# Narrow products as column tiles of the array: HGRN2's levels within 32 tokens and Mamba-2's chunk products

## The chip, the core and the metric

The kernel runs on one core of one Trainium2 chip. TensorE (PE) multiplies and writes to PSUM, VectorE (DVE) and ScalarE (ACT) do elementwise work, GpSimd (POOL) a few small operations, and SyncE (SP) issues nearly all transfers. The metric is the device time of one execution in microseconds, as the median of several runs.

## What is computed

The reference is an encoder trunk of two layers on 512 tokens of 1024 features. Layer 0 mixes tokens with HGRN2, layer 1 with Mamba-2, both in both directions, and each is followed by a gated channel mixer (ConvGLU). What the change touches are the products within a block of tokens:

```python
# HGRN2, one direction, per chunk (b = cumulated log of the forget gate)
rel = jnp.where(lower, b[t] - b[s], -inf)
att = jnp.einsum('bhtsk,bhsk->bhts', qc * jnp.exp(rel), kc)
o = o_inter + jnp.einsum('bhts,bhsv->bhtv', att, vc)
# Mamba-2, one direction, per chunk of 128
cb = jnp.einsum('bclgn,bcsgn->bgcls', cc, bc)
y_diag = jnp.einsum('bgjcls,bcsgjp->bclgjp', cb[:, :, None] * lmat, xd)
```

Everything is float32; HGRN2 has 8 heads of 128 channels, Mamba-2 32 heads of 64 channels in 8 groups.

## The kernel before

**Projections.** All large products take both operands split into two float32r parts and sum three products (`mm3`, lines 160 to 162), mostly 128 x 128 x 512. The weights come in pieces through `load`; ACT copies the high part (L134) and DVE subtracts the low part (L135).

**The order on TensorE** in the two mixers is written out by hand. A generator of projection work (`fill`) yields its cost, and `weave` inserts the steps of each head or group among it at given times (`HEADS` and `HSTEPS` for HGRN2, `MAMBA` and `STEPS` for Mamba-2). The orders on the other engines come from the framework's scheduler.

**HGRN2, a head (`mix(hd)`).** The tile `kq` holds four arrays of 128 channels x 512 tokens: the keys and queries of both directions. The attention within a block of 128 tokens is built by halving. The diagonal (`p0`, L537) and then levels m = 1, 2, 4, 8, 16, 32, 64 each take one step. At level m, ACT gathers into `km` the forward keys of each block's first half and the backward keys of the second (L545), TensorE multiplies it with the gathered queries over whole blocks of 128 x 128, four of them in one PSUM bank `pl` (L551), and of these DVE keeps with a masked copy those pairs that part at this level (L554 for the diagonal, L556), in the tile `at0` of 128 x 512. At m = 64 there is no mask: two products of 64 x 64 for each block go to the two halves of the partitions (L560, L562), and ACT copies them (L564, L565). After each level DVE multiplies the level's decays into `kq` in place (L574, L575), which the next level's gather and products wait for, and forms the decays of the doubled blocks (`tot`, L577). At the end `at0` is the left operand of the head's output (L612).

**Mamba-2, a group (`mix(g)`).** For each of four heads, `weights(j)` makes C B^T with decays and step sizes (ACT L879, DVE L881 and L883) as a tile E of 128 x 512, and L933 multiplies each block of 128 x 128 with the head's 64 channels of `x_t`, into 64 columns of `py`. L939 follows, the product with the states.

**Norms.** `stats` sums the squares over the channels with products against one column of ones (L225), after each mixer and channel mixer and in the last output.

Of the kernel before, what the change touches and what calls it, by code (L numbers as in the profile page):

```python
# [9 lines left out]
F32 = mybir.dt.float32  # L10
# [8 lines left out]
P = 128  # L19
T = 512  # L20
NB = T // P
# [10 lines left out]
# when HGRN2's heads are worked on among its projections, and the steps of a head, of 13 in all  # L32
HEADS = ((66, 136), (90, 170), (133, 209), (169, 250), (213, 292), (248, 315), (293, 353), (314, 368))
HSTEPS = (1, 1, 2, 3, 4, 5, 6, 7, 8.3, 9.5, 10, 11, 12)
# Mamba-2's work for TensorE, in order: a group's projections of B, C and x, its z, and parts of the output
MAMBA = [(c[0], int(c[1:])) for c in "p0 z0 p1 z1 p2 z2 o1 p3 o1 z3 o2 p4 z4 o2 p5 z5 o2 p6 z6 p7 z7 o8".split()]
# when the steps of a group's scan are issued among it, from the start of its projections
# [4 lines left out]
# artanh(s) = s (1 + z p(z)), z = s^2, to 4e-10 of it on |s| <= 1/3  # L42
# [3 lines left out]
def fl(t):  # L46
    """A tile [P, a, b] as [P, a*b]."""
    return t.rearrange("p a b -> p (a b)")


def view(ap, offset, dims):
    """The elements of ap's partitions at `offset` from its first, by [stride, size] pairs."""
    return bass.AP(tensor=ap.tensor, offset=ap.offset + offset, ap=[ap.ap[0], *dims])
# [3 lines left out]
def tile_trunk(ctx: ExitStack, tc: tile.TileContext, x, norm1_w, norm2_w, a_w_in, a_lb_logits, a_norm_w, a_w_out,  # L57
# [24 lines left out]
    # residual stream, channel-major, and the operand of the next projection split in two  # L82
# [22 lines left out]
    def bmask(m):  # L105
        return m.unsqueeze(1).to_broadcast([P, NB, P])

# [1 line left out]
    plan, ready = deque(), deque()  # L109

    def want(key, parts, nk):
        """Queues the columns of `parts` (APs of nk * 128 rows), side by side."""
        for k0 in range(0, nk, 4):
            plan.append((key, [x[k0 * P:min(nk, k0 + 4) * P] for x in parts]))
# [28 lines left out]
    def take(key, ahead=2):  # L143
        """The next weights in the plan, and those after them on their way."""
        got = []
        while (ready or plan) and (ready[0][0] if ready else plan[0][0]) == key:
            if not ready:
                k, parts = plan.popleft()
                ready.append((k, halves(*load(parts))))
            got.append(ready.popleft()[1])  # L150
        assert got, key
        fetch(ahead)

        def part(i, k, c0, n=P):
            return got[k // 4][i][:, k % 4, c0:c0 + n]

        return part
# [6 lines left out]
    # Streams of work for TensorE are generators that yield the time (in products of 128 x 128 x 512) of each piece.  # L164
    def proj_ch(p, w, c0):
        """Channel-major projection of the normalized stream (before its row scale): [128 features, T]."""
        yield from proj_chs([(p, w, c0)])

    def proj_chs(ps):
        """Several of them side by side, while the stream's tiles come in."""  # L170
        for k in range(ND):
            for p, w, c0 in ps:
                mm3(p, w(0, k, c0), w(1, k, c0), uhi[k], ulo[k], k == 0, k == ND - 1)
            if k % 2:
                yield 2 * len(ps)

    def proj_tok(p, w, blks):
        """Token-major projection of two blocks of tokens: [128 tokens, 2, 256 features]."""
        for i, b in enumerate(blks):
            bs = slice(b * P, b * P + P)  # L180
            for k in range(ND):
                mm3(p[:, i * 256:(i + 1) * 256], uhi[k][:, bs], ulo[k][:, bs], w(0, k, 0, 256), w(1, k, 0, 256),
                    k == 0, k == ND - 1)
                if k % 4 == 3:
                    yield 2

    def weave(fill, jobs, t=0):
        """Runs `fill`, and among it the steps of each job (steps, times), each at its time."""
        todo = sorted(((t, i) for i, (_, times) in enumerate(jobs) for t in times), reverse=True)
        for c in fill:  # L190
            t += c
            while todo and todo[-1][0] <= t:
                next(jobs[todo.pop()[1]][0], None)
        while todo:
            next(jobs[todo.pop()[1]][0], None)
# [24 lines left out]
    def stats(tmp, blocks=range(NB), more=()):  # L220
        """The tokens' scales, from the squares' sums and tiles of more squares."""
        pst = misc_ps()
        for b in blocks:
            for n, s in enumerate((ssum, *more)):
                PE.matmul(pst[:, b:b + 1], s[:, b * P:(b + 1) * P], ones[:, 0:1], start=n == 0, stop=n == len(more))  # L225
# [5 lines left out]
    def spread(tmp):  # L231
        """The tokens' scales along the free axis."""
# [7 lines left out]
    def out_proj(key, yhi, ylo, after):  # L240
        """h += w^T y, and `after` for each finished tile."""
# [98 lines left out]
    def first_masks():  # L340
        """Masks on [s, t] of a 128-block: the pairs that part at a level of halving."""
# [4 lines left out]
        xf = ip.tile([P, P], F32, name="xf")  # L346
        ge = ip.tile([P, P], F32, name="ge")
        V.tensor_tensor(mU, si, ti, ALU.is_le)
        V.tensor_tensor(si, si, ti, ALU.bitwise_xor)
        V.tensor_copy(xf, si)  # L350
        masks[0] = cst.tile([P, P], U8, name="m0")
        V.tensor_scalar(masks[0], xf, 0.0, None, ALU.is_equal)
        for m in (2, 4, 8, 16, 32):
            masks[m] = cst.tile([P, P], U8, name=f"m{m}")
# [3 lines left out]
    def params():  # L358
# [4 lines left out]
        # lower bounds of the forget gate: softmax over the layers' logits, first row  # L363
# [20 lines left out]
    def come(*ds):  # L384
        """Tiles of x, channel-major in PSUM."""
# [66 lines left out]
    def hgrn2():  # L452
# [66 lines left out]
        def mix(hd):  # L519
# [8 lines left out]
            # attention within blocks of 128, [s, t]; between them, states [k channel, v channel]  # L528
            at0 = t2k("at0", 2)
            diag = pv(at0)  # L530
# [4 lines left out]
            for b in range(NB):  # L535
                bs = slice(b * P, b * P + P)
                PE.matmul(p0[:, bs], ks[:, bs], q[:, bs], start=True, stop=True)  # L537
# [3 lines left out]
            while m < P:  # L541
                n2 = T // (2 * m)
                if m < 64:
# [3 lines left out]
                    pl = misc_ps()  # L547
                    for b in range(NB):
                        bs = slice(b * P, b * P + P)
                        qm = view(kq, T + b * P, [[2 * m, P // (2 * m)], [T + m, 2], [1, m]])  # L550
                        PE.matmul(pl[:, bs], km[:, bs], qm, start=True, stop=True)  # L551
                    if m == 1:
                        A.copy(diag, pv(pl))
                        V.copy_predicated(diag, bmask(masks[0]), pv(p0))  # L554
                    else:
                        V.copy_predicated(diag, bmask(masks[m]), pv(pl))  # L556
                else:
                    pl = misc_ps()
# [7 lines left out]
                # from blocks of m to blocks of 2m  # L566
# [14 lines left out]
            # tot: [P, 2, NB], products over blocks of 128; the blocks whose states the next ones (before, backward) take  # L581
# [23 lines left out]
            # output of the head, its norm and gate  # L605
# [26 lines left out]
        # a pair's projections take 80 units, the first six heads' output 48  # L632
# [71 lines left out]
    def mamba():  # L704
# [35 lines left out]
        def steps(x1):  # L740
            """Step sizes and cumulated decays: rows (half of the tokens, direction, head)."""
# [3 lines left out]
            # softplus: max(x, 0) + log1p(e), e = exp(-|x|); log1p(e) = 2 artanh(e / (2 + e)), at most 2 artanh(1/3)  # L745
# [88 lines left out]
        def h4(ap):  # L834
            """[P, n, 4 heads x 64] with the heads apart."""
            return ap.rearrange("p n (h e) -> p n h e", e=64)

        def mix(g):
            sb, sc, sx0, sx1, z = groups[g]
            hs = 4 * g  # L840
            # token-major x and B, and C B^T within the chunks as [s, l]
# [23 lines left out]
            def hv(t, c0, n, dr):  # L865
                """Per token and head, spread over a head's channels: [P, n, 4, 64]."""
                return t[:, c0:c0 + n, dr * NH + hs:dr * NH + hs + 4].unsqueeze(3).to_broadcast([P, n, 4, 64])

            def weights(j):
                """C B^T with the decays and step sizes of a head, as [s, l]."""  # L870
# [16 lines left out]
            # states at the chunks' borders  # L887
# [27 lines left out]
            # diagonal of the backward direction and the skip: one factor per token and head  # L915
# [10 lines left out]
            # within the chunks, a head at a time, and among them what the states give  # L926
            py = [misc_ps(), misc_ps()]
            for j in range(4):
                yield
                w = ws[j]  # L930
                for b in range(NB):
                    o = (b % 2) * 256 + j * 64
                    PE.matmul(py[b // 2][:, o:o + 64], w[:, b * P:(b + 1) * P], x_t[:, b, j * 64:(j + 1) * 64],  # L933
                              start=True, stop=True)
# [14 lines left out]
            # gate and group norm  # L949
# [68 lines left out]
        # a group's step begins with its projections of B, C and x (32 units, 8 more for the first group's dt)  # L1018
# [20 lines left out]
    def last_out(key, yhi, ylo, pool):  # L1039
        """The last products, the norm, and the output; the last tiles by halves of the tokens."""  # L1040
# [3 lines left out]
        def finish(d, p, ts, blocks):  # L1044
            """The tile's last steps; those of TensorE are left for later."""
# [79 lines left out]
```

## Time and profile before

| | |
|---|---|
| median of 3 runs | 1607.37 us (1607.34 to 1609.07) |
| profiled execution, span from first to last instruction | 1605.7 us |
| TensorE matmul busy / weight loads busy | 1589.4 / 1339.1 us |
| VectorE / ScalarE / GpSimd busy | 1060.1 / 773.5 / 27.4 us |
| matmuls | 8239 |
| HBM read / written | 147.70 / 2.23 MB |

The profile is of one execution, and its times are from its first instruction to its last; the median of the runs is 1.7 us above its span. Matmuls overlap in the array, so that their durations add up to more than the time they take: a matmul's price is the distance from its start to the next one's. A line such as L160 is that of the helper `mm3`, for all projections. The tensors' names in the rows are the program's: `pp` and `pm` are PSUM tiles of projections and of the rest.

### The profile page before, as it was taken

The page shows a single profiled execution, that of the slowest core. Times are in us where ns is not written, and L with a number is a line of the kernel's source. Part 1 is how long each engine was busy: PE and PEld are TensorE (multiplying, and loading weights), DVE is VectorE, ACT ScalarE, POOL GpSimd, SP SyncE. Part 2 cuts the span into 40 slices and gives each one's busy share as a digit, 9 for nine tenths or more (in the row PEclk, how much of TensorE's full clock was granted, in tenths as well). Part 3 has the DMA queues.
Part 4 walks back from the last instruction along what each step waited for, and adds up shares of the span by engine and source line. Part 5 has one row for each costly group of instructions (what it writes and reads, how often), then busy time and mean ns, then how long its engine had stood idle before and what let it go on. Part 6 is the DMA issues. An engine that isn't in the chain of part 4 may idle for free.

```text
span 1605.7 us, 21165 instructions
## 1 busy us (share of the span) xinstructions
PE 1589.4 (99%) x8239; PEld 1339.1 (83%) x8239; DVE 1060.1 (66%) x1652; ACT 773.5 (48%) x1356; POOL 27.4 (2%) x31
## 2 busy tenths in 40 slices
PE   8999999999999999999999999999999999999998
PEld 6889898987888888887888888888887888888887
DVE  6687677777655345545898888787878655246543
ACT  5445444535433123333589876667755333123333
POOL 0000000000000000000000000000000000000000
PEclk9999999999999999999999999999999999999999
DMA  5312222113232333323254334334313323233221
GB/s 180 101 53 67 66 66 66 47 44 113 87 101 83 105 92 92 99 79 99 77 172 135 116 109 119 120 93 117 101 47 118 96 89 105 79 105 95 82 81 71
DMA packets 153579, 151.31 MB, mean 94 GB/s; under 512 B 8374, under 2 KB 144263, under 8 KB 153479
## 3 DMA queue, kind: packets, MB, share of 16 engines
q1 hardware_dynamic: 153415, 149.93, 30.5%
q8 instruction: 65, 1.06, 0.3%
q14 instruction: 35, 0.29, 0.1%
q0 software_dynamic: 32, 0.02, 0.0%
q10 hardware_dynamic: 32, 0.01, 0.0%
HBM read 147.70 MB, written 2.23 MB: 93 GB/s over the span
## 4 chain that ended last, share of the span: by engine, by line
PE 51%; DVE 1%; issue 1%; ACT 0%; POOLq 0%; POOL 0%; ACTq 0%
PE pp L160 15%; PE pp L161 15%; PE pp L162 15%; PE pm L933 2%; PE pm L939 1%; PE pm L901 1%; PE pm L850 0%; PE pm L973 0%; PE pm L861 0%; PE pm L162 0%; PE pm L161 0%; PE pm L160 0%; PE pm L845 0%; PE pm L1054 0%; PE pm L237 0%
## 5 line engine op out<-in xcount | busy, mean ns | idle before, releaser
L160 PE MATMUL pp<-uhi,whi 128*128 128x512 f32 x1184 | 480.1, 406 | 0.0
L162 PE MATMUL pp<-uhi,wlo 128*128 128x512 f32 x1184 | 469.2, 397 | 0.3 <-DVE wlo L135 0.3
L161 PE MATMUL pp<-ulo,whi 128*128 128x512 f32 x1184 | 469.3, 396 | 0.0
L134 ACT CAST whi<-raw 128x1024 fp32r<-128x1024 f32 (+1 forms) x258 | 259.5, 1006 | 329.0 <-PE pp L161 256.5
L135 DVE TENSOR_TENSOR wlo<-raw,whi 128x1024 fp32r<-128x1024 f32 (+1 forms) x258 | 301.3, 1169 | 154.3 <-ACT whi L134 153.3
L162 PEld LDWEIGHTS pp<-uhi,wlo 128*128 128x128 f32 x1184 | 223.0, 188 | 55.3 <-DVE wlo L135 1.2
L161 PEld LDWEIGHTS pp<-ulo,whi 128*128 128x128 f32 x1184 | 223.4, 189 | 51.1 <-issue 0.5
L160 PEld LDWEIGHTS pp<-uhi,whi 128*128 128x128 f32 x1184 | 223.0, 188 | 50.9 <-issue 0.5
L160 PE MATMUL pp<-yh,whi 128*128 128x512 f32 (+1 forms) x500 | 196.2, 392 | 0.9 <-ACT whi L134 0.9
L161 PE MATMUL pp<-yl,whi 128*128 128x512 f32 (+1 forms) x500 | 192.1, 384 | 0.0
L162 PE MATMUL pp<-yh,wlo 128*128 128x512 f32 (+1 forms) x500 | 191.3, 383 | 0.0
L160 PE MATMUL pp<-whi,uhi 128*128 128x256 f32 x384 | 111.2, 290 | 0.0
L160 PEld LDWEIGHTS pp<-yh,whi 128*128 128x128 f32 x500 | 93.9, 188 | 20.5 <-ACT whi L134 1.3
L162 PEld LDWEIGHTS pp<-yh,wlo 128*128 128x128 f32 x500 | 93.8, 188 | 19.3
L161 PEld LDWEIGHTS pp<-yl,whi 128*128 128x128 f32 x500 | 94.0, 188 | 18.2
L162 PE MATMUL pp<-whi,ulo 128*128 128x256 f32 x384 | 108.3, 282 | 0.0
L252 DVE TENSOR_TENSOR h<-h,pp 128x512 f32<-128x512 f32 x80 | 54.2, 684 | 81.6 <-PE pp L162 80.9
L161 PE MATMUL pp<-wlo,uhi 128*128 128x256 f32 x384 | 108.0, 281 | 0.0
L879 ACT ACTIVATE E<-R,col_t 128x128 f32<-128x128 f32 x256 | 81.9, 391 | 27.7 <-PE pm L933 22.2
L659 ACT ACTIVATE c<-gp,colp 128x512 f32<-128x512 f32 x44 | 35.7, 817 | 101.2 <-DVE gp L657 101.2
L661 DVE SCALAR_TENSOR_TENSOR c<-gp,colp,c 128x512 f32<-128x512 f32 x88 | 65.6, 750 | 20.8 <-ACT c L659 19.4
L161 PEld LDWEIGHTS pp<-wlo,uhi 128*128 128x128 f32 x384 | 72.6, 189 | 0.5
(272 smaller groups left out, 1992.5 us busy)
## 6 DMA issues: line engine op xcount, KB each, us to landing
raw<-in_ffn_w_in_dram SPq DMA_DIRECT2D x88, 512.0 KB, 3.5
raw<-in_a_w_in_dram SPq DMA_DIRECT2D x40, 512.0 KB, 3.5
raw<-in_ffn_w_out_dram SPq DMA_DIRECT2D x40, 512.0 KB, 3.3
raw<-in_b_w_in_dram SPq DMA_DIRECT2D x32, 512.0 KB, 3.7
R<-ac_d SPq DMA_DIRECT2D x64, 256.0 KB, 3.6
raw<-in_b_w_in_dram SPq DMA_DIRECT2D x32, 256.0 KB, 3.3
raw<-in_b_w_out_dram SPq DMA_DIRECT2D x12, 512.0 KB, 3.3
xt<-in_x_dram SPq DMA_DIRECT2D x4, 512.0 KB, 7.8
```

The costliest lines, as they stand in the source:

```text
L134: A.copy(hi[:, :nk, :c0], r)
L135: V.tensor_tensor(lo[:, :nk, :c0], r, hi[:, :nk, :c0].bitcast(F32), ALU.subtract)
L160: PE.matmul(dst, lhi, rhi, start=start, stop=False)
L161: PE.matmul(dst, lhi, rlo, start=False, stop=False)
L162: PE.matmul(dst, llo, rhi, start=False, stop=stop)
L252: V.tensor_tensor(h[d], h[d], p, ALU.add)
L659: A.activation(c, g[:, 0:T], AF.Identity, scale=col(W_FW[l], f), bias=col(W_FB, l * NFF + f))
L661: V.scalar_tensor_tensor(c, g[:, k:k + T], col(W_FW[l], k * NFF + f), c, ALU.mult, ALU.add)
L879: A.activation(e[:, bs], r[:, bs], AF.Identity, bias=col_t[:, b, dr * NH + hd:dr * NH + hd + 1])
L901: PE.matmul(dst, b_t[:, dr + c, :], xds[dr][:, c, :], start=True, stop=True)
L933: PE.matmul(py[b // 2][:, o:o + 64], w[:, b * P:(b + 1) * P], x_t[:, b, j * 64:(j + 1) * 64], start=True, stop=True)
L939: PE.matmul(po[:, i * 256:(i + 1) * 256], sc[:, c * P:(c + 1) * P], hin[dr][:, c - 1 if dr == 0 else c, :], start=True, stop=True)
```

## The change

The products whose result is wanted only in a narrow strip are made as narrow strips, each in its own column tile of the array: a product with 32 (or 64) columns of the stationary operand, whose result goes to 32 (or 64) partitions of PSUM that begin at a multiple of 32 (or 64).

- HGRN2's diagonal and levels 1 to 16: 16 products of 32 x 32 instead of 4 of 128 x 128, into 128 columns of the bank instead of 512 (`strips`). The masks become 128 x 32, the masked copies 128 x 128, into a new tile `atd`.
- Level 32: no mask and no gather; four products for each block (`half`), each with the keys of 32 tokens and the queries of the 32 beside them. Four ACT copies bring them into `at0`, and four DVE copies bring `atd` onto its diagonal.
- Mamba-2's L933: two products of 64 columns for each block instead of one of 128.
- `stats`: four products of 32 columns instead of one of 128.

```diff
+Q = 32
     def bmask(m):
-        return m.unsqueeze(1).to_broadcast([P, NB, P])
+        return m.unsqueeze(1).to_broadcast([P, NB, m.shape[1]])
...
             for n, s in enumerate((ssum, *more)):
-                PE.matmul(pst[:, b:b + 1], s[:, b * P:(b + 1) * P], ones[:, 0:1], start=n == 0, stop=n == len(more))
+                for j in range(0, P, Q):
+                    PE.matmul(pst[j:j + Q, b:b + 1], s[:, b * P + j:b * P + j + Q], ones[:, 0:1],
+                              start=n == 0, stop=n == len(more))
...
-        xf = ip.tile([P, P], F32, name="xf")
-        ge = ip.tile([P, P], F32, name="ge")
+        xf = ip.tile([P, Q], F32, name="xf")
+        ge = ip.tile([P, Q], F32, name="ge")
...
+        si, ti = si[:, 0:Q], ti[:, 0:Q]
         V.tensor_tensor(si, si, ti, ALU.bitwise_xor)
+        V.tensor_scalar(si, si, Q - 1, None, ALU.bitwise_and)
...
-        for m in (2, 4, 8, 16, 32):
-            masks[m] = cst.tile([P, P], U8, name=f"m{m}")
+        for m in (2, 4, 8, 16):
+            masks[m] = cst.tile([P, Q], U8, name=f"m{m}")
...
-            diag = pv(at0)
+            atd = pool.tile([P, NB, Q], F32, tag="atd", name="atd", bufs=2)
+            def strips(lhs, rhs, p):
+                for b in range(NB):
+                    for j in range(0, P, Q):
+                        PE.matmul(p[j:j + Q, b * Q:(b + 1) * Q], lhs(b * P + j), rhs(b * P + j), start=True, stop=True)
+            def pq(p):
+                return p[:, 0:P].rearrange("p (a b) -> p a b", b=Q)
...
-            for b in range(NB):
-                bs = slice(b * P, b * P + P)
-                PE.matmul(p0[:, bs], ks[:, bs], q[:, bs], start=True, stop=True)
+            strips(lambda o: ks[:, o:o + Q], lambda o: q[:, o:o + Q], p0)
...
-                if m < 64:
+                pl = misc_ps()
+                if m < Q:
                     km = t2k("km", 2)
                     A.copy(km.rearrange("p (a b c) -> p a b c", b=2, c=m),
                            view(kq, 0, [[2 * m, n2], [3 * T + m, 2], [1, m]]))
-                    pl = misc_ps()
+                    strips(lambda o: km[:, o:o + Q],
+                           lambda o: view(kq, T + o, [[2 * m, Q // (2 * m)], [T + m, 2], [1, m]]), pl)
+                    if m == 1:
+                        A.copy(atd, pq(pl))
+                        V.copy_predicated(atd, bmask(masks[0]), pq(p0))
+                    else:
+                        V.copy_predicated(atd, bmask(masks[m]), pq(pl))
+                elif m == Q:
+                    half = ((0, KF, QF, Q), (Q, KB, QB, 0), (2 * Q, KF, QF, 3 * Q), (3 * Q, KB, QB, 2 * Q))
                     for b in range(NB):
-                        bs = slice(b * P, b * P + P)
-                        qm = view(kq, T + b * P, [[2 * m, P // (2 * m)], [T + m, 2], [1, m]])
-                        PE.matmul(pl[:, bs], km[:, bs], qm, start=True, stop=True)
-                    if m == 1:
-                        A.copy(diag, pv(pl))
-                        V.copy_predicated(diag, bmask(masks[0]), pv(p0))
-                    else:
-                        V.copy_predicated(diag, bmask(masks[m]), pv(pl))
+                        for j, k, r, t in half:
+                            PE.matmul(pl[j:j + Q, b * Q:(b + 1) * Q], kq[:, k, b * P + j:b * P + j + Q],
+                                      kq[:, r, b * P + t:b * P + t + Q], start=True, stop=True)
+                    for j, k, r, t in half:
+                        A.copy(pv(at0[j:j + Q])[:, :, t:t + Q], pq(pl)[j:j + Q])
+                    for j in range(0, P, Q):
+                        V.tensor_copy(pv(at0[j:j + Q])[:, :, j:j + Q], atd[j:j + Q])
...
-                    PE.matmul(py[b // 2][:, o:o + 64], w[:, b * P:(b + 1) * P], x_t[:, b, j * 64:(j + 1) * 64],
-                              start=True, stop=True)
+                    for i in (0, 64):
+                        PE.matmul(py[b // 2][i:i + 64, o:o + 64], w[:, b * P + i:b * P + i + 64],
+                                  x_t[:, b, j * 64:(j + 1) * 64], start=True, stop=True)
```

(The diff also drops comments and docstrings.) On TensorE the places of the blocks stay as they are. Here in HGRN2, before, with the first block pair of one head (L537, L551) and level 32 of another (the second L551) among the projections:

```order
L162 MATMUL pp<-uhi_84,wlo 128x512
L537 MATMUL pm<-q,km 128x128 x4
L551 MATMUL pm<-kq,km 128x128 x4
L160 MATMUL pp<-uhi_85,whi 128x512
L161 MATMUL pp<-ulo_93,whi 128x512
L162 MATMUL pp<-uhi_85,wlo 128x512
L160 MATMUL pp<-uhi_86,whi 128x512
L161 MATMUL pp<-ulo_94,whi 128x512
L162 MATMUL pp<-uhi_86,wlo 128x512
L551 MATMUL pm<-kq,km 128x128 x4
```

and after, where L541 is the product in `strips`, L572 that of level 32, and L161 to L163 are `mm3`:

```order
L163 MATMUL pp<-uhi_84,wlo 128x512
L541 MATMUL pm<-q,km 32x32 x16
L541 MATMUL pm<-kq,km 32x32 x16
L161 MATMUL pp<-uhi_85,whi 128x512
L162 MATMUL pp<-ulo_93,whi 128x512
L163 MATMUL pp<-uhi_85,wlo 128x512
L161 MATMUL pp<-uhi_86,whi 128x512
L162 MATMUL pp<-ulo_94,whi 128x512
L163 MATMUL pp<-uhi_86,wlo 128x512
L572 MATMUL pm<-kq 32x32 x16
```

Each block keeps its place; its 4 products become 16. In Mamba-2, before:

```order
L161 MATMUL pp<-ulo_94,whi 128x512
L162 MATMUL pp<-uhi_86,wlo 128x512
L933 MATMUL pm<-xt,E_6556 128x64 x4
L939 MATMUL pm<-hin,sc 128x256
L160 MATMUL pp<-uhi_87,whi 128x512
L161 MATMUL pp<-ulo_95,whi 128x512
```

and after, where L954 follows L933:

```order
L162 MATMUL pp<-ulo_94,whi 128x512
L163 MATMUL pp<-uhi_86,wlo 128x512
L954 MATMUL pm<-xt,E_7298 64x64 x8
L960 MATMUL pm<-hin,sc 128x256
L161 MATMUL pp<-uhi_87,whi 128x512
L162 MATMUL pp<-ulo_95,whi 128x512
```

The eight narrower products stand where the four were. On DVE, at a head's level 16 and 32, before (`at_699` is this head's `at0`, `m_186` and `m_189` are the masks of levels 16 and 32; the rows with F and `at_905` are another head's):

```order
L556 COPY_PREDICATED at_699<-m_186,pm 128x512
L574 TENSOR_TENSOR kq<-kq,tot_828 128x32x16
L575 TENSOR_TENSOR kq<-kq,tot_828 128x32x16
L474 TENSOR_TENSOR pr<-pp,rbc 128x512
L135 TENSOR_TENSOR wlo<-raw,whi 128x1024
L478 TENSOR_TENSOR q<-pr,sg__876 128x512
L574 TENSOR_TENSOR kq<-kq,F 128x512
L554 COPY_PREDICATED at_905<-m_175,pm 128x512
L575 TENSOR_TENSOR kq<-kq,F 128x512
L556 COPY_PREDICATED at_699<-m_189,pm 128x512
L574 TENSOR_TENSOR kq<-kq,tot_866 128x16x32
L575 TENSOR_TENSOR kq<-kq,tot_866 128x16x32
```

and after, where `atd` takes the masked copies, L577 is the copy from it to `at0`, and L594 and L595 are the products into `kq`:

```order
L566 COPY_PREDICATED atd<-m_187,pm 128x128
L594 TENSOR_TENSOR kq<-kq,tot_887 128x32x16
L595 TENSOR_TENSOR kq<-kq,tot_887 128x32x16
L479 TENSOR_TENSOR pr<-pp,rbc 128x512
L136 TENSOR_TENSOR wlo<-raw,whi 128x1024
L483 TENSOR_TENSOR q<-pr,sg__947 128x512
L594 TENSOR_TENSOR kq<-kq,F 128x512
L564 COPY_PREDICATED atd<-m_176,pm 128x128
L595 TENSOR_TENSOR kq<-kq,F 128x512
L577 COPY at_697<-atd 32x4x32 x4
L594 TENSOR_TENSOR kq<-kq,tot_937 128x16x32
L595 TENSOR_TENSOR kq<-kq,tot_937 128x16x32
```

At level 32 four copies stand ahead of the products into `kq` in place of the masked copy.

More of the change, by code (lines that the diff above doesn't have):

```diff
@@ L345, in first_masks @@
         G.iota(ti, pattern=[[1, P]], base=0, channel_multiplier=0)
-        xf = ip.tile([P, P], F32, name="xf")
-        ge = ip.tile([P, P], F32, name="ge")
+        xf = ip.tile([P, Q], F32, name="xf")
+        ge = ip.tile([P, Q], F32, name="ge")
         V.tensor_tensor(mU, si, ti, ALU.is_le)
+        si, ti = si[:, 0:Q], ti[:, 0:Q]
         V.tensor_tensor(si, si, ti, ALU.bitwise_xor)
+        V.tensor_scalar(si, si, Q - 1, None, ALU.bitwise_and)
         V.tensor_copy(xf, si)
-        masks[0] = cst.tile([P, P], U8, name="m0")
+        masks[0] = cst.tile([P, Q], U8, name="m0")
         V.tensor_scalar(masks[0], xf, 0.0, None, ALU.is_equal)
-        for m in (2, 4, 8, 16, 32):
-            masks[m] = cst.tile([P, P], U8, name=f"m{m}")
+        for m in (2, 4, 8, 16):
+            masks[m] = cst.tile([P, Q], U8, name=f"m{m}")
             V.tensor_scalar(ge, xf, float(m), None, ALU.is_ge)
@@ L546, in mix @@
                            view(kq, 0, [[2 * m, n2], [3 * T + m, 2], [1, m]]))
-                    pl = misc_ps()
-                    for b in range(NB):
-                        bs = slice(b * P, b * P + P)
-                        qm = view(kq, T + b * P, [[2 * m, P // (2 * m)], [T + m, 2], [1, m]])
-                        PE.matmul(pl[:, bs], km[:, bs], qm, start=True, stop=True)
-                    if m == 1:
-                        A.copy(diag, pv(pl))
-                        V.copy_predicated(diag, bmask(masks[0]), pv(p0))
-                    else:
-                        V.copy_predicated(diag, bmask(masks[m]), pv(pl))
+                    strips(lambda o: km[:, o:o + Q],
[7 more added lines that the diff above has]
+                    half = ((0, KF, QF, Q), (Q, KB, QB, 0), (2 * Q, KF, QF, 3 * Q), (3 * Q, KB, QB, 2 * Q))
+                    for b in range(NB):
+                        for j, k, r, t in half:
[5 more added lines that the diff above has]
+                        V.tensor_copy(pv(at0[j:j + Q])[:, :, j:j + Q], atd[j:j + Q])
                 else:
-                    pl = misc_ps()
                     for b in range(NB):
```

## The prediction

> **What bounds the kernel.** I read the page's shares first, then the chain of work that ended last, then the stages by windows.
>
> ```profile
> PE 1589.4 (99%) x8239; PEld 1339.1 (83%) x8239; DVE 1060.1 (66%) x1652; ACT 773.5 (48%) x1356; POOL 27.4 (2%) x31
> PE 51%; DVE 1%; issue 1%; ACT 0%; POOLq 0%; POOL 0%; ACTq 0%
> 60.00:360.00 300.00, 299.93 (x1907) 263.92 (x1906) 223.13 (x375) 135.01 (x284) 7.43 (x7) 1.00 0.20 61
> 780.00:1220.00 440.00, 438.62 (x2521) 383.60 (x2520) 368.29 (x637) 323.72 (x657) 9.87 (x8) 1.00 0.37 111
> ```
>
> The first row says that TensorE (PE) is busy 99% of the span; the second that the chain is almost all PE. The last two rows are the stages that the change touches, HGRN2 (60 to 360 us) and Mamba-2 (780 to 1220 us); after the stretch's length come the busy us of PE, its weight loads, DVE and ACT. PE has no idle time in either, at a granted clock of 1.00, while DVE has 77 us to spare in the first and 72 in the second. So a product's price is the time by which it pushes back the projection products behind it, and what the change saves or adds there goes straight into the end.
>
> The groups that the change narrows, kept apart by shape:
>
> ```profile
> L551 PE MATMUL pm<-kq,km 128*128 128x128 f32 x384 | 54.9, 287 | 0.1
> L933 PE MATMUL pm<-xt,E 128*128 128x64 f32 x256 | 32.1, 268 | 0.5 <-DVE E L883 0.5
> L537 PE MATMUL pm<-q,km 128*128 128x128 f32 x64 | 8.4, 275 | 0.0
> L225 PE MATMUL pm<-ones,ssum 128*128 128x1 f32 x32 | 4.2, 239 | 0.0
> L225 PE MATMUL pm<-ones,sq 128*128 128x1 f32 x8 | 1.5, 253 | 0.8 <-ACT sq L215 0.8
> ```
>
> The trace has two matmuls for each float32 product. With 8 heads, L551 is 6 blocks of 8 matmuls a head and L537 one; L933 is 32 blocks of 8; the norms' sums (L225) are 40 matmuls, worth five blocks of 8. Durations overlap, so I price a block by starts: from the last projection matmul ahead of it to the second behind it, less those two matmuls' own pitch.
>
> **The price of what goes.** A wide block of HGRN2, PE's timeline:
>
> ```profile
> 102.96 0.39 PE L162 MATMUL pp<-uhi,wlo 128*128 128x512 f32 x1
> 103.19 1.05 PE L551 MATMUL pm<-kq,km 128*128 128x128 f32 x8
> 104.00 0.48 PE L160 MATMUL pp<-uhi,whi 128*128 128x512 f32 x1
> 104.32 0.40 PE L161 MATMUL pp<-ulo,whi 128*128 128x512 f32 x1
> ```
>
> 104.32 - 102.96 is 1.36; the pitch of the 512-wide products is 0.23 (102.96 to 103.19), so the block costs 1.36 - 0.46 = 0.90 us, 0.112 a matmul. The first two blocks of a head come together, and the second (level m = 1, whose moving operand is gathered in single elements) is dearer:
>
> ```profile
> 133.37 0.28 PE L162 MATMUL pp<-whi,ulo 128*128 128x256 f32 x1
> 133.49 1.05 PE L537 MATMUL pm<-q,km 128*128 128x128 f32 x8
> 134.38 1.49 PE L551 MATMUL pm<-kq,km 128*128 128x128 f32 x8
> 135.56 0.42 PE L160 MATMUL pp<-whi,uhi 128*128 128x256 f32 x1
> 135.82 0.28 PE L161 MATMUL pp<-wlo,uhi 128*128 128x256 f32 x1
> ```
>
> 135.82 - 133.37 less two pitches of 0.12 is 2.21 us for the pair: 0.89 for L537, 1.32 for m = 1, which is 0.165 a matmul instead of 0.112.
>
> **The price of what comes.** The kernel already has one product in column tiles: level 64, two halves of 64 columns (L560, L562).
>
> ```profile
> 252.77 0.39 PE L161 MATMUL pp<-ulo,whi 128*128 128x512 f32 x1
> 253.00 0.40 PE L162 MATMUL pp<-uhi,wlo 128*128 128x512 f32 x1
> 253.33 0.27 PE L560 MATMUL pm<-kq 128*64 128x64 f32 x1
> 253.34 0.27 PE L562 MATMUL pm<-kq 128*64 128x64 f32 x1
> 253.44 0.22 PE L560 MATMUL pm<-kq 128*64 128x64 f32 x1
> ...
> 253.61 0.22 PE L560 MATMUL pm<-kq 128*64 128x64 f32 x1
> 253.62 0.22 PE L562 MATMUL pm<-kq 128*64 128x64 f32 x1
> 253.67 0.22 PE L560 MATMUL pm<-kq 128*64 128x64 f32 x1
> ...
> 253.79 0.22 PE L562 MATMUL pm<-kq 128*64 128x64 f32 x1
> 253.94 0.50 PE L160 MATMUL pp<-uhi,whi 128*128 128x512 f32 x1
> 254.28 0.39 PE L161 MATMUL pp<-ulo,whi 128*128 128x512 f32 x1
> ```
>
> Three readings. The halves run side by side: the second starts 0.01 us after the first, and the next pair 0.06 after that. The pair's pitch of about 0.058 against 0.112 at 128 wide fits 0.005 + 0.00084 a column, so the array, not the issue, sets it. And getting in and out costs: the 16 matmuls would take 8 x 0.058 = 0.47, but the block costs 254.28 - 253.00 - 0.46 = 0.82, so 0.35 goes into the change of shape (L560 starts 0.33 after L162 instead of 0.23, L161 0.34 after L160).
>
> *HGRN2.* Each of the seven blocks of a head (L537, m = 1 to 32) becomes 16 products of 32 columns, 32 matmuls for 8. For one block, between these ends:
> - Low: four tiles run together as two do. By the fit a 32-wide matmul has a pitch of 0.032; eight rounds are 0.26; entry and exit 0.33, a little less than for 64 as the matmuls are shorter: 0.59.
> - High: issue is the limit, at the 0.029 that a matmul of the half block took on average (0.46 / 16): 32 x 0.029 = 0.93, with 0.33 1.26, dearer than the 0.90 that goes.
> - I take 0.70, nearer the low end: 0.01 from one tile's start to the next shows that issue can be faster than 0.029, which was what the array let through; but no row shows 32 matmuls at that rate, so I add 0.11.
>
> For the pair at a head's beginning, low: 0.33 + 0.26 + 8 x 0.046 (m = 1's dearer elements, 0.165 / 0.112 of 0.032) = 0.96; high: 0.33 + 64 x 0.029 = 2.19. I take 1.35, the longer run being likelier to outrun the issue. So 8 x (2.21 - 1.35) = 6.9 us and, for m = 2 to 32, 40 x (0.90 - 0.70) = 8.0 us.
>
> *Mamba-2.*
>
> ```profile
> 855.64 0.39 PE L162 MATMUL pp<-uhi,wlo 128*128 128x512 f32 x1
> 855.87 1.00 PE L933 MATMUL pm<-xt,E 128*128 128x64 f32 x8
> 856.71 0.65 PE L939 MATMUL pm<-hin,sc 128*128 128x256 f32 x2
> 857.01 0.59 PE L160 MATMUL pp<-uhi,whi 128*128 128x512 f32 x1
> 857.43 0.40 PE L161 MATMUL pp<-ulo,whi 128*128 128x512 f32 x1
> ```
>
> 857.43 - 855.64 - 0.46 = 1.33, of which the two of L939 (256 wide, so twice 0.112) are 0.45: 0.88 for the eight of L933, although they stream only 64 columns; their 128-column weights set the pitch. The new block is the half block's shape exactly, 16 matmuls of 64 by 64: 0.82. Gain 0.06, taken as 0.08 since other half blocks are a shade cheaper; times 32, 2.6 us. Ends: 0 and 0.12 a block.
>
> *Norms' sums.* Five blocks of 8 matmuls, one column each:
>
> ```profile
> 393.24 0.39 PE L162 MATMUL pp<-uhi,wlo 128*128 128x512 f32 x1
> 393.46 0.95 PE L225 MATMUL pm<-ones,ssum 128*128 128x1 f32 x8
> 394.27 0.47 PE L160 MATMUL pp<-uhi,whi 128*128 128x512 f32 x1
> 394.59 0.40 PE L161 MATMUL pp<-ulo,whi 128*128 128x512 f32 x1
> ```
>
> 1.35 - 0.46 = 0.89 each, against 0.70: 5 x 0.19 = 1.0 us.
>
> *DVE and ACT.*
>
> ```profile
> L556 DVE COPY_PREDICATED at<-m,pm 128x512 f32<-128x512 uint8 x40 | 29.6, 741 | 13.7 <-PE pm L551 13.6
> L545 ACT COPY km<-kq 128x512 f32<-128x512 f32 x47 | 31.4, 668 | 62.6 <-DVE kq L575 56.7 <-PE pm L551 4.7 <-PE pm L537 1.0
> L597 ACT COPY sd<-pm 128x128 f32<-128x128 f32 x16 | 4.1, 265 | 5.8 <-PE pm L594 5.7
> ```
>
> The masked copies shrink to a quarter of the columns, and one a head goes with a km copy; at m = 32 four ACT copies and four DVE copies come, about 0.27 each by the L597 row (for DVE a guess from the same row): per head ACT gains 0.67 and loses 1.1, DVE gains 0.74 and loses 1.1, and saves some 0.4 in each of five masked copies. Both have the room, so I cost it at nothing. Queued behind DVE's four copies are the two products that make kq for level 64, and PE's level 64 waits for those; were they late by a whole 1.1 us, a head would lose that much, 9 us in all. The smaller masks at the start hide behind the input's loads. No DMA is added; the order of some of SP's loads of R shifts.
>
> Sum: 6.9 + 8.0 + 2.6 + 1.0 = 18.5 us. The profiled span is 1605.7 and the median of the runs 1607.4, so 1.7 us lie around the span and stay. 1607.4 - 18.5 = **1589 us**. All low ends together give 8 x 1.25 + 40 x 0.31 + 3.8 + 1.5 = 27.7, 1580 us.
>
> **Rivals.**
> - *Issue-bound strips; ends slower.* HGRN2 has four times the matmuls in each block. If each needs 0.029, the sum is 40 x (0.90 - 1.26) + 8 x (2.21 - 2.19) + 2.6 + 5 x (0.89 - 1.26) = -13.5: 1621 us. In terms of the time p per matmul the gain is 43 - 1952 p us, so it turns at p = 0.022. For it: nothing shows a longer dense run. Against it: starts 0.01 apart. The Trainium skill, TensorEngine Tiling (Array Packing), section Instruction Overhead, speaks for this rival: each matmul costs about 60 cycles however few its columns, so no tiling factor should be taken from a dimension that is already small; its page TensorE: Matmul & The Clock Gate, section Back-to-back issue gap, puts that at about 25 ns, and by it the sum would be an estimated loss of 6 us, 1613. The trace disagrees for matmuls of different tiles, whose starts are 0.01 apart. 0.12.
> - *The four strips do not run together*, so that the change does not do what it says: 32 x 0.032 + 0.33 = 1.35 a block, and 40 x -0.45 + 8 x -0.6 + 2.6 - 2.3 = -22: 1629 us. The pairs of L560 and L562 speak against it. 0.03.
> - *Two at a time*, since two is all the trace shows: 16 rounds of 0.032 make 0.84 a block and 1.6 a first pair: 40 x 0.06 + 8 x 0.6 + 2.6 + 0.3 = 10: 1597 us. 0.15.
> - *The saved time turns into waits.* Shorter blocks bring a head's steps closer; the loop from block to block is DVE's masked copy, two products and ACT's km copy. PE waited for km three times in all, so there is little slack known; and the changed order on DVE, ACT and SP in Mamba-2, where DVE is busy 84%, could make PE wait for E. One us lost in each of the eight heads and eight groups is 16 and eats the gain: about 1605. 0.08.
>
> **How the numbers follow.** The forecast has 0.62, with its own range 1580 to 1596. Its side is faster; so is two at a time (0.15), and half of the waits' case (0.04): 0.81. Within 0.2% (3.2 us, about what a measurement of this kernel can tell from no change): the other half and the turning point of the issue, 0.05. Slower: 0.14. The range of 1578 to 1603 leaves out the slower cases and those of no change, and reaches below the low ends by 2 us.
>
> **What would show it.** In the changed trace the groups of 32 by 32 should start in fours some 0.01 apart and a block cost 0.6 to 0.8 us by the same subtraction; L933's successor 0.8; the masked copies a third of 741 ns; PE still at 99%. I am wrong if a strip block takes over 0.9 us (issue), if its matmuls start evenly 0.03 apart, if PE shows new idle time before the strips or before level 64, or if entry and exit cost much more than 0.35.

## The result, and the profile after

| kernel | median | lowest and highest of the runs | ratio to before, 95% interval |
|---|---|---|---|
| before | 1607.36 us | 1606.77 to 1609.07 | |
| changed | 1566.04 us | 1563.51 to 1567.89 | 0.9737 [0.9724, 0.975] |

The change gains 41.3 us, more than twice the 18.4 that was forecast, and ends below the range. Two causes of about equal size are behind that: the narrow blocks, near the low end of their estimate, and one which no term of the prediction contains.

The profile of the changed kernel: busy times and the shares of the chain from the page, then the same two stages by windows (after the stretch's length the busy us of PE, its weight loads, DVE, ACT and POOL, then granted clock, DMA share and GB/s).

```profile
span 1566.1 us, 24651 instructions
PE 1544.3 (99%) x9959; PEld 1287.7 (82%) x9959; DVE 1042.7 (67%) x1675; ACT 776.9 (50%) x1382; POOL 27.2 (2%) x31
PE 49%; DVE 2%; ACT 1%; issue 1%; POOL 0%; POOLq 0%; ACTq 0%
```

```profile
60.00:360.00 300.00, 297.87 (x3378) 245.99 (x3376) 220.02 (x421) 147.85 (x334) 8.17 (x8) 1.00 0.22 70
780.00:1220.00 440.00, 434.75 (x2745) 368.66 (x2744) 365.62 (x619) 323.05 (x651) 11.94 (x9) 0.99 0.37 111
```

PE is still the bound at 99%; 1720 more matmuls stand in a span that is 39.6 us shorter. In Mamba-2's window PE is now idle for 5.2 us instead of 1.4, at a clock a shade below 1.

PE's timeline, changed kernel: a strip block of HGRN2 (L541, the 32 matmuls of 128 x 32), the first pair of a head, a norm's sum and a half block of Mamba-2, each between projection products (L161 to L163).

```profile
100.70 0.39 PE L163 MATMUL pp<-uhi,wlo 128*128 128x512 f32 x1
101.02 0.46 PE L541 MATMUL pm<-kq,km 128*32 128x32 f32 x32
101.41 0.50 PE L161 MATMUL pp<-uhi,whi 128*128 128x512 f32 x1
101.74 0.39 PE L162 MATMUL pp<-ulo,whi 128*128 128x512 f32 x1
...
129.65 0.28 PE L163 MATMUL pp<-whi,ulo 128*128 128x256 f32 x1
129.86 0.46 PE L541 MATMUL pm<-q,km 128*32 128x32 f32 x32
130.13 0.56 PE L541 MATMUL pm<-kq,km 128*32 128x32 f32 x32
130.62 0.39 PE L161 MATMUL pp<-whi,uhi 128*128 128x256 f32 x1
130.85 0.28 PE L162 MATMUL pp<-wlo,uhi 128*128 128x256 f32 x1
...
371.10 0.39 PE L163 MATMUL pp<-uhi,wlo 128*128 128x512 f32 x1
371.42 0.43 PE L227 MATMUL pm<-ones,ssum 128*32 128x1 f32 x32
371.78 0.50 PE L161 MATMUL pp<-uhi,whi 128*128 128x512 f32 x1
372.12 0.40 PE L162 MATMUL pp<-ulo,whi 128*128 128x512 f32 x1
...
875.87 0.40 PE L163 MATMUL pp<-uhi,wlo 128*128 128x512 f32 x1
876.20 0.69 PE L954 MATMUL pm<-xt,E 128*64 128x64 f32 x16
876.81 0.70 PE L960 MATMUL pm<-hin,sc 128*128 128x256 f32 x2
877.16 0.58 PE L161 MATMUL pp<-uhi,whi 128*128 128x512 f32 x1
877.58 0.39 PE L162 MATMUL pp<-ulo,whi 128*128 128x512 f32 x1
```

By the prediction's subtraction, with the pitches of this trace (0.227 at 512 columns, 0.12 at 256): the strip block costs 101.74 - 100.70 - 0.454 = 0.59 us, the first pair 0.96, the norm's sum 0.57, and the half block 1.256 - 0.45 = 0.81. The 32 starts of a strip block (single records) lie 6 to 7 ns apart within a round of four and 11 to 12 from round to round (33 once, behind the first round), so a round takes 0.0315 us and the block 0.26; entry and exit are the other 0.33.

What the prediction did not look at is how the 512-wide projection products follow each other where nothing stands between them. The first and the last of ten such products, before, and then in the changed kernel:

```profile
1250.11 0.40 PE L160 MATMUL pp<-uhi,whi 128*128 128x512 f32 x1
...
1252.22 0.39 PE L160 MATMUL pp<-uhi,whi 128*128 128x512 f32 x1
```

```profile
1250.31 0.39 PE L161 MATMUL pp<-uhi,whi 128*128 128x512 f32 x1
...
1252.35 0.39 PE L161 MATMUL pp<-uhi,whi 128*128 128x512 f32 x1
```

Nine pitches take 2.11 us before and 2.04 after: 0.234 against 0.227, for the same kind of product, with `uhi` or `ulo` as the moving operand, at a granted clock of 1.00. The program has 5244 products of 512 columns; where one follows another directly, the distances from start to start sum to 18.8 us less than before. The distances at the blocks sum to 20.3 us less (235.4 to 215.1), with the new waits in them. The 256-wide projection products, nearly all of which have `uhi` or `ulo` as weights, keep their pitch: 151.3 us in all before and 151.1 after.

### The profile page after: what moved, and what is told of

It is laid out like the page before. It is cut to its first block, busy times and chain, and to the rows that moved or that the text cites. A ratio compares the mean times of both kernels' runs of the same rounds, so it can differ in the third digit from the quotient of the medians.

```text
span 1566.1 us, 24651 instructions
## 1 busy us (share of the span) xinstructions
PE 1544.3 (99%) x9959; PEld 1287.7 (82%) x9959; DVE 1042.7 (67%) x1675; ACT 776.9 (50%) x1382; POOL 27.2 (2%) x31
## 4 chain that ended last, share of the span: by engine, by line
PE 49%; DVE 2%; ACT 1%; issue 1%; POOL 0%; POOLq 0%; ACTq 0%
PE pp L161 14%; PE pp L163 14%; PE pp L162 14%; PE pm L960 2%; PE pm L954 1%; PE pm L921 1%; PE pm L870 0%; PE pm L994 0%; PE pm L881 0%; PE pm L163 0%; PE pm L161 0%; PE pm L162 0%; PE pm L865 0%; PE pm L1075 0%; ACT whi L135 0%
## 5 line engine op out<-in xcount | busy, mean ns | idle before, releaser
L161 PE MATMUL pp<-uhi,whi 128*128 128x512 f32 x1184 | 474.7, 401 | 0.0
L163 PE MATMUL pp<-uhi,wlo 128*128 128x512 f32 x1184 | 462.6, 391 | 0.3 <-DVE wlo L136 0.3
L162 PE MATMUL pp<-ulo,whi 128*128 128x512 f32 x1184 | 462.7, 391 | 0.0
L163 PEld LDWEIGHTS pp<-uhi,wlo 128*128 128x128 f32 x1184 | 222.8, 188 | 48.9 <-DVE wlo L136 1.2
L161 PEld LDWEIGHTS pp<-uhi,whi 128*128 128x128 f32 x1184 | 223.1, 188 | 46.1 <-issue 0.5
L161 PE MATMUL pp<-yh,whi 128*128 128x512 f32 (+1 forms) x500 | 197.2, 394 | 0.9 <-ACT whi L135 0.9
L163 PE MATMUL pp<-yh,wlo 128*128 128x512 f32 (+1 forms) x500 | 191.8, 384 | 0.0
L161 PE MATMUL pp<-whi,uhi 128*128 128x256 f32 x384 | 111.3, 290 | 0.0
L163 PEld LDWEIGHTS pp<-yh,wlo 128*128 128x128 f32 x500 | 93.8, 188 | 20.3
L161 PEld LDWEIGHTS pp<-yh,whi 128*128 128x128 f32 x500 | 94.0, 188 | 18.9 <-ACT whi L135 1.3
L162 PEld LDWEIGHTS pp<-yl,whi 128*128 128x128 f32 x500 | 93.9, 188 | 18.8
L163 PE MATMUL pp<-whi,ulo 128*128 128x256 f32 x384 | 108.6, 283 | 0.0
L161 PEld LDWEIGHTS pp<-whi,uhi 128*128 128x128 f32 x384 | 73.4, 191 | 0.9
```

What stands on the lines that cost most here:

```text
L161: PE.matmul(dst, lhi, rhi, start=start, stop=False)
L162: PE.matmul(dst, lhi, rlo, start=False, stop=False)
L163: PE.matmul(dst, llo, rhi, start=False, stop=stop)
```

## The experiments

**Theory.** The six masks of 128 bytes (a partition) became five of 32. They stand last among the constants, so everything allocated behind them, the weights `whi` and `wlo` and the pools, moved down by 608 bytes, while the moving operands `uhi` and `ulo` ahead of them stayed. By the addresses in the built programs, the moving operand less the weights is 160 bytes modulo 256 before the change and 0 after it. Products are faster by where their operands lie. **Rivals:** the shorter narrow blocks let PE or its weight loads run faster; the changed schedule relieves a collision with DVE, ACT or DMA.

**1. The masks' bytes given back.** `pad` stands behind the last constant, in the changed kernel with n = 608, and in the kernel before with n = 32 and 64:

```diff
     olb = cst.tile([P, 8], F32, name="olb")
+    pad = cst.tile([P, n // 4], F32, name="pad")
+    V.memset(pad, 0.0)
```

> The changed kernel with an unused tile of 608 bytes behind the constants, the room that its smaller masks gave up, so that the weights lie where they lay before. Phase theory: the pitch goes back to about 234 ns and the time up by 20 to 25 us: 1586 to 1591 us; what is left of the gain is that of the strips, about 1607 - 1588 = 19 us. Strips theory: 1566 us as after the change, pitch 227 ns.

> The kernel before, with one unused tile of 32 bytes a partition behind the constants, so that the weights' tiles and the mixers' pools begin 32 bytes later; the products stay as they were. Phase theory: a projection product is fast when the addresses of its two operands within a partition differ by a multiple of 64 bytes (uhi and whi then do; before they are 32 off). 3672 products of 512 columns with uhi or ulo go from a pitch of about 234 to 227 ns, some 20 to 25 us: 1583 to 1588 us. Strips theory (the projections are faster after the change because the strips leave TensorE, PSUM or the other engines less busy): no change, 1607 us.

> The same with 64 bytes. Phase theory: uhi and whi are still 32 bytes off, so no change: 1607 us, pitch 234 ns. Rival (any other place of the weights, or a certain distance, helps): 1583 to 1588 us. Strips theory: 1607 us.

Measured: the changed kernel with 608 bytes 1584.62 us (1582.46 to 1584.92), ratio to before 0.9858 [0.9841, 0.9874]; before with 32 bytes 1602.95, 0.9968 [0.9957, 0.998]; with 64 bytes 1605.81, 0.9989 [0.9979, 0.9998]. PE's timeline with the 608 bytes, ten such products at the same time of the run:

```profile
1250.26 0.40 PE L163 MATMUL pp<-uhi,whi 128*128 128x512 f32 x1
...
1252.37 0.40 PE L163 MATMUL pp<-uhi,whi 128*128 128x512 f32 x1
```

The pitch is back at 0.234, with every narrow block still in place: the addresses make it, not the blocks or the schedule. So 18.6 us of the gain belong to the addresses and 22.7 to the narrow blocks. But 32 bytes, which brought the distance of `uhi` and weights to a multiple of 64, gave 4 us and not 19: the rule that was expected, a period of 64 bytes, fell.

**2. Both moved by 32.** The same `pad`, and another of 32 bytes ahead of `uhi`, behind `h`.

> The kernel before with two tiles of 32 bytes, one ahead of uhi and one behind the constants: uhi moves by 32 and the weights by 64 bytes, so that both begin at a multiple of 64. Phase theory in its relative form: fast, 1583 to 1588 us. Its absolute form (the weights must begin 32 bytes past a multiple of 64, as after the change): 1607 us. Strips theory: 1607 us.

Measured: 1603.08 us, 0.9972 [0.9962, 0.9982], as with 32 bytes behind the constants alone. That fits neither 64 bytes of distance nor an absolute place; what the two kernels have in common is the distance (moving operand less weights): 384 bytes modulo 512, which is 128 modulo 256, and slow.

**3. The mended rule.** The rule now expected was a period of 512 bytes. Before, with n = 416 (`uhi` and weights at the same place modulo 512, as in the changed kernel) and n = 160 (256 apart, so slow if the period is 512); and the changed kernel with a pad first in the pool of the ConvGLU (`padf`) and one first in that of Mamba-2 (`padm`), so that `yh` and `yl`, the moving operands of the output projections, too lie a multiple of 512 from the weights:

```diff
+        padf = pool.tile([P, 112], F32, name="padf")
+        V.memset(padf, 0.0)
...
+        padm = pool.tile([P, 120], F32, name="padm")
+        V.memset(padm, 0.0)
```

> The kernel before with an unused tile of 416 bytes behind the constants: uhi and the weights then begin at the same place modulo 512 bytes, as after the change. Phase theory, mended by the last runs (not 64 bytes count, but the distance modulo 512, the length of a 128-column row of float32 weights: 0 is fast): pitch of the uhi products 234 to 228 ns, and 1607.3 - 18.6 = 1589 us, from what after_pad608 gave back. Rival (a smaller unit plus something that the change itself brings, as 32 bytes gave only 4 us): 1603 us as with 32 bytes.

> The same with 160 bytes: uhi and the weights are 256 bytes apart modulo 512. Phase theory with a unit of 512: slow or in between, 1600 to 1607 us. With a unit of 256 or less: fast, 1589 us.

> The changed kernel with two unused tiles, of 448 bytes at the start of ConvGLU's pool and of 480 at the start of Mamba-2's, so that the operands of the output projections (yh, yl) also begin with the weights modulo 512 bytes; they were 64 and 32 off. Phase theory: ConvGLU's 1380 output products go from 229.0 to 227.8 ns and Mamba-2's 384 from about 233.3 to 227.8, 1.7 + 2.1 = 4 us: 1562 us. Rival (the distance counts only for uhi, whose products read other tiles in turn): 1566 us.

Measured: 1587.48 us, 0.9877 [0.986, 0.9893]; 1586.91, 0.9873 [0.9858, 0.9888]; and 1562.08, 0.9719 [0.9705, 0.9734]. The first came out as expected; the second is as fast, so the period is not 512 but 256, and 128 is slow by experiment 2. The third gains 4.0 us by the medians, and in its trace the output products follow each other every 227 ns instead of 229 (ConvGLU) and 233 (Mamba-2). (Its expectation counts 1380 output products for the ConvGLU; that is all of them, and 996 are the ConvGLU's, so that its sum should have been 3.3 us and not 4.) PE's timeline of the kernel before with 416 bytes:

```profile
1249.89 0.39 PE L162 MATMUL pp<-uhi,whi 128*128 128x512 f32 x1
...
1251.93 0.39 PE L162 MATMUL pp<-uhi,whi 128*128 128x512 f32 x1
```

0.227, and 20 us less for a kernel in which TensorE's instructions and their order are the same, and their addresses alone differ. Over the kernels, counting pairs of 512-wide products with no block between and less than 0.3 us apart, by the addresses in the built programs:

| distance modulo 256 | 0 | 32 | 64 | 96 | 128 | 160 |
|---|---|---|---|---|---|---|
| mean pitch, ns | 227.6 | 233.2 | 229.0 | 233.4 | 232.4 | 234.2 |

The columns 32 and 64 come from output products alone. That the distance decides is shown by adding bytes alone. Why it does, no run here tells; nor whether a product's own weights or the next one's count, since all weights here begin at the same place modulo 256.

**4. Does the gain of the strips need the four tiles in turn?** The changed kernel with the loops of `strips` swapped; addresses and instructions stay:

```diff
-                for b in range(NB):
-                    for j in range(0, P, Q):
+                for j in range(0, P, Q):
+                    for b in range(NB):
```

> The changed kernel with the two loops of the strips swapped: the four blocks of tokens of one column tile follow each other, instead of the four tiles of one block of tokens; every address and every instruction stays. Theory A (each tile works in program order, and only neighbours in the queue that lie in different tiles run side by side): 32 products of a block go one after the other at the 0.031 us that a round of four took, so 32 x 0.031 + 0.33 = 1.33 instead of 0.60, the first pair 32 x 0.031 + 32 x 0.046 + 0.33 = 2.8 instead of 0.97: 40 x 0.73 + 8 x 1.8 = 44 us more, about 1610. Theory B (TensorE looks ahead and fills the tiles out of order): no change, 1566. Theory C (the gain of a strip block is its fewer streamed columns and not that four run together): no change either.

Measured: 1587.28 us, 0.9868 [0.9854, 0.9881], 21.2 more than the changed kernel. PE's timeline of the swapped kernel:

```profile
102.91 0.39 PE L163 MATMUL pp<-uhi,wlo 128*128 128x512 f32 x1
103.23 0.90 PE L541 MATMUL pm<-kq,km 128*32 128x32 f32 x32
104.06 0.50 PE L161 MATMUL pp<-uhi,whi 128*128 128x512 f32 x1
104.39 0.39 PE L162 MATMUL pp<-ulo,whi 128*128 128x512 f32 x1
```

The block costs 1.03 instead of 0.59, and the first pair 1.81. 32 x 0.44 + 8 x 0.85 = 20.9, close to the measured loss; L572 and the norms' sums were not swapped. Theories B and C fall, and theory A holds in direction. Its price was too high, 0.022 a matmul and not 0.031. The starts (single records) show why: at both ends of a block they lie about 32 ns apart, but nine of the 31 distances are only 4 to 10 ns. That fits three matmuls of one tile running beside the first three of the next at each of the three changes of tile, though the trace doesn't name the tiles. In this order 1.03 is more than the 0.90 of the wide block: HGRN2's strips would have gained 32 x (0.90 - 1.03) + 8 x (2.21 - 1.81) = -1 us. The order of two loops is the whole gain of these levels. The Trainium skill, TensorE: Matmul & The Clock Gate, section The mechanism, has matmuls start in strict order, and the run agrees: were any waiting product started first, swapping the loops would not have cost 21 us.

**5. Mamba-2's halves alone.** L954's block is 0.07 us cheaper, yet PE waits (the waits view: us in total, times, longest), in the changed kernel and then before:

```profile
PE pm L954 <- DVE E L903: 4.1, 2, 3.4
PE pm L240 <- DVE dg L238: 3.4, 2, 3.1
```

```profile
PE pm L237 <- DVE dg L235: 2.2, 1, 2.2
PE pm L933 <- DVE E L883: 0.5, 1, 0.5
```

The wait for dg (L240, in the first norm) is not the halves' doing: it is 3.1 us too in the kernel before with 416 bytes, and 1.3 in the changed kernel with 608. At each of the two long waits of the changed kernel the clock halves (timeline, and the two windows behind the waits, columns as in the windows above):

```profile
836.84 1.12 PE L954 MATMUL pm<-xt,E 128*64 128x64 f32 x16 [3.37 <-DVE E L903]
837.90 2.08 PE L960 MATMUL pm<-hin,sc 128*128 128x256 f32 x4
839.41 0.99 PE L161 MATMUL pp<-uhi,whi 128*128 128x512 f32 x1
840.20 0.63 PE L162 MATMUL pp<-ulo,whi 128*128 128x512 f32 x1
```

```profile
34.00:41.00 7.00, 6.73 (x15) 4.64 (x16) 3.87 (x12) 3.76 (x7) 0.00 (x0) 0.54 0.00 1
836.00:842.70 6.70, 5.86 (x27) 4.76 (x28) 6.70 (x11) 5.62 (x15) 0.00 (x0) 0.50 0.75 210
```

Two runs separate the halves from the rest, with the edit of the diff at L933 undone in the changed kernel, and made alone in the kernel before with the 416 bytes:

> The changed kernel with Mamba-2's products as before, 128 columns in one. If the halves are worth what the blocks' subtraction says, 0.07 us in each of 32 blocks, this is 2.2 us slower: 1568 us. If the halves only move the end of a stage that waits for DVE (TensorE waited for E at 836 us for 3.4 us in the changed kernel and its granted clock fell to 0.5 behind it), the time is the same or up to 5 us shorter: 1561 to 1566 us.

> The kernel before with the 416 bytes behind the constants (weights and moving operand a multiple of 256 bytes apart; measured 1587.5) and of the change only Mamba-2's halves. Theory A (a half block costs 0.07 us less in any case): 32 x 0.07 = 2.2 us less, about 1585.3. Theory B (the halves bring PE closer to ACT and DVE in Mamba-2, and a wait for E with a stretch at half the clock follows, as in the changed kernel): 3 to 5 us lost against those 2.2, so 1586 to 1591, with idle time of PE on E that the kernel before does not have.

Measured: without the halves 1563.04 us (1562.75 to 1563.99), 0.9725 [0.971, 0.9739], so 3.0 less than with them; the halves alone 1587.45, 0.9874 [0.986, 0.9887], the same as the 1587.48 without. The waits of that kernel, and of the one with the 416 bytes and without the halves:

```profile
PE pm L936 <- DVE E L885: 4.2, 2, 3.3
```

```profile
PE pm L935 <- DVE E L885: 1.1, 1, 1.1
```

A wait of 3.2 to 3.4 us for E stands in all five kernels with the halves, and in none of the nine without them, where the longest is 1.1. It takes back the 2.2 us that the cheaper blocks save: that is the second pair of runs. The 3.0 us of the first pair hang on the clock. In the kernel with the 416 bytes and the halves the granted clock stays at 1.00 behind the same wait (window as above):

```profile
856.80:863.60 6.80, 6.77 (x57) 5.51 (x57) 6.70 (x10) 5.09 (x15) 0.00 (x0) 1.00 0.78 236
```

And the four runs of the changed kernel go from 1563.51 us at a mean granted clock of 0.998 to 1567.89 at 0.995, the one profiled; the fastest is no slower than the kernel without the halves (1562.75 to 1563.99). So the halves gain nothing, and lose some 3 us where the clock halves behind their wait. They also change the scheduler's order on DVE and ACT in many places; which of these moves makes that one E late was not taken apart.

**6. A better version.** First the changed kernel with experiment 3's pads and without the halves; then that one with the norm's `spread` moved behind the twelve products that follow it, to fill PE's wait for dg (L240):

```diff
+        first_products(1, 6, 2, w)
         spread(ip)
         run(lower)
-        first_products(1, 6, 2, w)
```

> The changed kernel with both corrections at once: the pools of the ConvGLU and of Mamba-2 moved by 448 and 480 bytes (measured 1562.1 alone) and Mamba-2's product 128 wide again (measured 1563.0 alone). Theory A (the two act on different stages and add up): 1566.0 - 4.0 - 3.0 = 1559. Theory B (the wait for E comes back as soon as Mamba-2's projections are faster): 1562.

> The kernel with both corrections, and the spreading of the first norm's scales moved behind the twelve products that follow it, so that PE has 2.7 us of work while DVE makes dg. Theory A (PE's 3.1 us of idle time there set the 6.8 us at half the clock): idle time falls to 0.4 us, no half clock, so 2.7 + 3 = about 5 us less than the one without it, about 1554. Theory B (the half clock comes from elsewhere, and only the idle time goes): 2.7 us less, about 1556. Theory C (the heads' first steps, which wait for rbc, come 2.7 us later and PE waits for them instead): no gain, 1559.

Measured: 1559.92 us (1559.61 to 1560.88), 0.97 [0.9687, 0.9713], 6.1 less than the changed kernel and the fastest here; the two corrections add up but for 1 us. With `spread` moved 1561.18, 0.9708 [0.9695, 0.9722]: no gain, as theory C said. PE's timeline of this kernel:

```profile
34.76 1.12 PE L240 MATMUL pm<-dg,ones 128*128 128x512 f32 x2
38.57 0.47 PE L161 MATMUL pp<-uhi,whi 128*128 128x512 f32 x1 [2.68 <-DVE pr L479]
```

The wait for dg is gone, and 2.68 us of waiting for DVE to empty a PSUM tile stand behind it: that step needs rbc, which now comes later. The wait was moved, not removed.

## Why the prediction was wrong

- **The step that failed is the sum itself.** It lists what the change does to the narrow blocks and takes 1607.4 less that, so everything else keeps its duration. The smaller masks were costed by the time to make them ("hide behind the input's loads") and not by the bytes that they free. That missing term measured 18.6 us by the changed kernel with and without the 608 bytes, and 20.1 by the kernel before with and without the 416. With it alone the forecast would have been about 1570.
- **The strips: mechanism right, size low.** 0.70 was taken for a block and 0.59 measured, the low end: issue keeps up at 0.008 a matmul, and the 0.11 added for doubt was not needed. m = 2 to 32 gave 40 x 0.31 = 12.4 instead of 8.0, the first pairs 8 x 1.25 = 10.0 instead of 6.9, the norms' sums 5 x 0.32 = 1.6 instead of 1.0. The fit through two shapes (0.032 a round) and the 0.33 for entry and exit were right.
- **Mamba-2: price right, sum wrong.** The block fell from 0.88 to 0.81 as forecast, 2.2 us; but by the medians the halves cost 3.0 net in the changed kernel and gain nothing alone. This is the fourth rival (saved time turns into waits, E in Mamba-2) at one place, with a stretch at half the clock, in some runs, that it didn't price.
- **Summed up:** 12.4 + 10.0 + 1.6 + 2.2 = 26.2 for the blocks against 18.5 forecast, close to the 27.7 of all low ends. With the addresses 18.6, that is 44.8; 41.3 was measured, which leaves 3.5 for the waits and the half clock of experiment 5.
- **The rivals:** issue-bound strips and two at a time are out by the starts 6 to 12 ns apart, and strips that don't run together by the block's 0.59 instead of 1.35. The Trainium skill's sixty cycles a matmul (TensorEngine Tiling (Array Packing), Instruction Overhead) don't hold between column tiles: 32 matmuls with their weight loads in 0.26 us. Its 4 ns or so for each further tile (TensorE: Matmul & The Clock Gate, section Measured speedup vs the span model) is near what this trace shows, and would have been the better page to weigh.
- **DVE and ACT** cost next to nothing in HGRN2, as taken: PE waited 0.7 us in all for km. The masked copy fell to 0.40 of its time rather than a third:

```profile
L566 DVE COPY_PREDICATED atd<-m,pm 128x128 f32<-128x128 uint8 x32 | 9.5, 297 | 5.6 <-PE pm L541 5.5
```

## What to carry to other kernels

A change that alters the size of any tile moves every tile allocated behind it; where one kind of product fills the span, read its steady pitch first, compare it with the same product in other kernels, and try a few bytes of padding before working on the rare shapes. Column tiles paid here when successive products went to different tiles; a long run pays more than a short one, since getting in and out (0.33 us) cost more than a block's work (0.26). A saving on the engine that bounds is only kept if its inputs come earlier too: look for the one wait it uncovers, and for what that does to the clock.

## What the hardware showed that was not expected

- The pitch of 512-wide float32r products depends on the distance between the moving operand and the weights in memory, modulo 256 bytes: 227.6 ns at 0, 229.0 at 64, 232 to 234 at the other distances seen. In a kernel with 5244 of them that is some 19 to 20 us, 1.2% of the span.
- PE's clock can be halved by quite short waits, but is not each time. Waits from 2.29 us (before, 32 bytes) to 3.38 us (the kernel with the output operands moved) came with a stretch at 0.5 that began between 1.4 us ahead of their end and 1.0 behind it, and near the start of a run one of 1.75 us did (`spread` moved); waits of 2.21 us (before), 3.19 us (changed, 608 bytes) and 3.35 us (before, 416 bytes and halves) did not. A stretch lasted 3.41 or 6.83 us. The Trainium skill, TensorE: Matmul & The Clock Gate, section What's actually happening, puts the idle window at about 3.4 us; here less sufficed. What decides between two waits of a length, these runs don't show.
- One column tile of 32 takes a matmul about every 32 ns while its products follow each other (the swapped kernel), and four tiles in turn take one every 8 ns (the changed one).
